# A ring of raw weight blocks in eight quarters instead of two whole blocks, in a one-core hybrid decoder layer

## The chip, the cores and the metric

The kernel runs on one core of one Trainium2 chip. The metric is the time of one execution on the device in microseconds, as a median of several runs; less is better. Beside the timed runs there is one profiled execution, whose trace is read here. The engines are named as in the profile: PE is TensorE, DVE is VectorE, ACT is ScalarE, POOL is GpSimd, SP is SyncE. SP issues most DMA transfers and computes nothing.

## What is computed

One layer of a decoder on 512 positions of width 1024, all in float32: an RMS norm, one wide input projection, two token mixers beside each other (a short gated convolution and a chunked gated delta rule with eight heads), a sigmoid-gated merge, an output projection, and a gated feed-forward part with a convolution over three positions.

```python
h = rmsnorm(x, norm_mix_g[l])
proj = h @ w_in[l]
bg, cg, xv, q, k, v, z, a, b, ga, gb = jnp.split(proj, pts, axis=-1)
y_a = short_conv_branch(bg, cg, xv, conv_a_w[l]) @ w_a_out[l]
y_b = gdn_branch(q, k, v, z, a, b, ...) @ w_b_out[l]
mix = jax.nn.sigmoid(ga) * y_a + jax.nn.sigmoid(gb) * y_b
x = x + mix @ w_o[l]
h = rmsnorm(x, norm_ffn_g[l])
x = x + conv_ffn(h, w_up[l], ffn_conv_w[l], w_down[l])
...
return rmsnorm(x, norm_final_g)
```

Nearly all of the arithmetic is in the products with `w_in`, `w_a_out`, `w_b_out`, `w_o`, `w_up` and `w_down`. Every weight is read from HBM once.

## The kernel before

**Products in three parts.** A float32 product is made of three matmuls in a rounded format (float32r): each operand is split into a rounded part and the rest (`wh` and `wl` for a weight, likewise for the activations), and `mm3` sums low x high, high x low and high x high (line 108 is the matmul in it).

**Blocks and jobs.** The weights are cut into blocks of 1 MB: 128 partitions by 16 tiles of 128 columns, or by four rows of 512. A list of jobs goes through them in order; `run_jobs` works one job at a time. A job has a block and a function `use` that issues its matmuls. There are three kinds of blocks:

- `Block`: four quarters, each split into `wh` (a cast on ACT, line 140) and `wl` (a subtraction on DVE, line 141).
- `SumBlock`: the block is used in a product scheme with seven instead of eight partial products. Its split has seven steps: quarters 0, 1 and 2 are split first ("11", "12", "22"), then DVE forms sums and differences in place in the same quarters (line 161, `to`), and four more parts are split from these: s3 from quarter 3, s2 from quarter 0, s4 from quarter 1 and s1 from quarter 2.
- `FormBlock`: rows for the products with `w_o` and `w_down`, loaded in one or two pieces (line 193). Those of `w_down` from the third on lie in buffers of their own (`raws`) and don't go through the ring.

**The ring.** The raw blocks lie in a ring with the tag `raw`: two slots of a whole block (16 KB a partition in all). A block is loaded by one DMA transfer of 1 MB on SP's queue (line 135). The tile framework lets a new tile into a slot when the last reader of the old tile is done, and places the waits itself. The first block (K of the first pair of heads) is already loaded in four pieces (line 419), into one tile. `wh` and `wl` have rings of `WQ` = 12 quarters each.

**The order.** In `run_jobs`, for job i: what is left of the split of block i is finished, the split of block i+1 is put into a queue that advances a step after every 2048 columns of matmuls, the load of block i+2 is issued, and then the matmuls of block i are issued. With these matmuls go the other queues' steps: PSUM results are taken out by ACT and DVE (in a `sum_job`, the copies `u` and `v` on lines 323 to 330 by ACT and the sums on lines 312 and 316 by DVE; the job's own later matmuls wait for the copies), and the delta rule's chains advance. The instructions of DVE, ACT, POOL and SP are put in order by a planner that simulates the engines and the transfers; in stretches under `manual_schedule` their order is the written one. Each engine, and SP's queue, works strictly in its order.

**The gate.** POOL issues a second kind of transfers, the sums of blocks of `w_o` and `w_down` that are formed in DRAM by accumulating transfers of 256 KB (line 1162). They are let in three at a time by `feed`, after each job from the middle of the kernel on: POOL copies one element of the raw block just being loaded (line 222), which makes it wait for the landing.

Of the kernel before, what the change touches and what calls it, by code (L numbers as in the profile page):

```python
# [9 lines left out]
F32 = mybir.dt.float32  # L10
F32R = mybir.dt.float32r
AF = mybir.ActivationFunctionType
ALU = mybir.AluOpType
# [3 lines left out]
P = 128  # L17
S = 512
# [8 lines left out]
C_BG, C_CG, C_XV, C_Q, C_K, C_V, C_Z, C_GA, C_GB = range(0, 36, 4)  # L27
# [33 lines left out]
def layer_kernel(ctx, tc, x, norm_mix_g, w_in, w_ab, conv_a_w, gdn_conv_w, gdn_A_log, gdn_dt_bias,  # L61
                 gdn_norm_g, w_a_out, w_b_out, w_o, norm_ffn_g, w_up, ffn_conv_w, w_down,
                 norm_final_g, out):
    nc = tc.nc
    pe, act, dve, pool = nc.tensor, nc.scalar, nc.vector, nc.gpsimd
# [6 lines left out]
    wp = ctx.enter_context(tc.tile_pool(name="wp", bufs=2))  # L72
# [3 lines left out]
    def nm(s):  # L76
        cnt[0] += 1
        return f"{s}{cnt[0]}"
# [8 lines left out]
    def advance(queue, n):  # L87
        while n and queue:
            queue[0].step()
            if queue[0].done:  # L90
                queue.popleft()
            else:
                n -= 1
# [28 lines left out]
            mm(o, ah, bh, False, i == n - 1, free)  # L122


    class Block:
        def __init__(self, src, quarter=(4, P)):
            self.src, self.quarter = src, quarter
            self.raw, self.ready, self.lead, self.fed = None, False, 2, True
            self.wh, self.wl = {}, {}

        def load(self):
            if self.raw is not None:
                return
            self.raw = wp.tile([P, 4, *self.quarter], F32, tag="raw", bufs=2, name=nm("raw"))
            nc.sync.dma_start(out=self.raw, in_=self.src())

        def part(self, name, src):
            wh = self.wh[name] = wp.tile([P, *self.quarter], F32R, tag="wh", bufs=WQ, name=nm("wh"))
# [4 lines left out]
        def split(self):  # L143
            if self.ready:
                return
            self.ready = True
            for q in range(4):
                self.part(q, self.raw[:, q])
                yield


# [1 line left out]
    class SumBlock(Block):  # L153
        def split(self):
            if self.ready:
                return
            self.ready = True
            r = [self.raw[:, q] for q in range(4)]

            def to(q, a, b, op):  # L160
                dve.tensor_tensor(out=r[q], in0=a, in1=b, op=op)  # L161

            self.part("11", r[0])
            yield
            self.part("12", r[1])
            yield
            self.part("22", r[2])
            yield
            to(2, r[3], r[2], ALU.add)
            to(3, r[0], r[3], ALU.subtract)  # L170
            self.part("s3", r[3])
            yield
            to(0, r[2], r[0], ALU.subtract)
            self.part("s2", r[0])
            yield
            to(1, r[1], r[0], ALU.subtract)
            self.part("s4", r[1])
            yield
            self.part("s1", r[2])
            yield  # L180


    class FormBlock(Block):
# [4 lines left out]
        def load(self):  # L188
            if self.raw is not None:
                return  # L190
            self.raw = self.place()
            for lo, hi, src in self.runs:
                nc.sync.dma_start(out=self.raw[:, lo:hi], in_=src)

        def split(self):
            if self.ready:
                return
            self.ready = True
            for q, name in enumerate(self.names):
                self.part(name, self.raw[:, q])  # L200
                yield

    def run_jobs(jobs):
        jobs[1][0].load()
        for i, (block, use) in enumerate(jobs):
            Task(block.split()).finish()
            drain(splits)
            if i + 1 < len(jobs):
                splits.append(Task(jobs[i + 1][0].split()))
            for j, (later, _) in enumerate(jobs[i + 2:i + 5]):  # L210
                if later.lead >= j + 2:
                    later.load()
            if adds and i + 2 < len(jobs) and jobs[i + 2][0].fed:
                feed(jobs[i + 2][0].raw)
            use(block.wh, block.wl)
# [2 lines left out]
    gate = const.tile([1, 64], F32, name="gate")  # L218

    def feed(raw):  # L220
        el = raw[0:1, 1].rearrange("p k n -> p (k n)") if len(raw.shape) == 4 else raw[0:1, 1]
        tc.keep_in_program_order(pool.tensor_copy(out=gate[:, 0:1], in_=el[:, 0:1]))  # L222
        advance(adds, FEED)

# [188 lines left out]
    tbd = [dram.tile([4, 8, 32, 32], F32, name=f"tbd{p}") for p in range(4)]  # L413

    k_block = Block(lambda: w_in[C_K])
    k_block.raw = wp.tile([P, 4, 4, P], F32, tag="raw", bufs=2, name=nm("raw"))

    def load_k(q):
        nc.sync.dma_start(out=k_block.raw[:, q], in_=w_in[C_K][:, 4 * q:4 * q + 4])

    HS = S // 2

# [6 lines left out]
    def ab_split():  # L429
        raw = ab_raw  # L430
        act.copy(out=ab2[:, :, 0:16], in_=raw)
        dve.tensor_tensor(out=ab2[:, :, 16:32], in0=raw, in1=ab2[:, :, 0:16].bitcast(F32), op=ALU.subtract)
# [44 lines left out]
    with tc.tile_pool(name="st1", bufs=1) as st1:  # L477
# [15 lines left out]
        load_x(0)  # L493
        load_x(1)
        load_k(0)
        wr = st1.tile([P, P], F32, name="wr")
        nc.sync.dma_start(out=wr[0:96], in_=gdn_conv_w.rearrange("o j (c p) -> (o j c) p", p=P))
        nc.sync.dma_start(out=wr[96:120], in_=conv_a_w.rearrange("o j (c p) -> (o j c) p", p=P))
        nc.sync.dma_start(out=wr[120:128], in_=norm_mix_g.rearrange("o (c p) -> (o c) p", p=P))
        ab_raw = st1.tile([P, ND, 16], F32, name="ab_raw")  # L500
        nc.sync.dma_start(out=ab_raw, in_=w_ab)
        load_k(1)
        load_x(2)
        load_x(3)
        load_k(3)
        load_k(2)
        dtb = gs.tile([P, H], F32, name="dtb")
# [54 lines left out]

        def round_k(q):
            wh = k_block.wh[q] = wp.tile([P, 4, P], F32R, tag="wh", bufs=WQ, name=nm("wh"))
            act.copy(out=wh, in_=k_block.raw[:, q])

        def rest_k(q):
            wl = k_block.wl[q] = wp.tile([P, 4, P], F32R, tag="wl", bufs=WQ, name=nm("wl"))
            dve.tensor_tensor(out=wl, in0=k_block.raw[:, q], in1=k_block.wh[q].bitcast(F32), op=ALU.subtract)


        def ab_tile(k):
# [11 lines left out]
        with tc.manual_schedule(engines={mybir.EngineType.DVE, mybir.EngineType.Activation, mybir.EngineType.Pool}):  # L584
# [4 lines left out]
            pe.transpose(out=po[:, 0:P], in_=wr, identity=ident)  # L589
            norm_x(1)  # L590
            round_k(0)
            dve.tensor_copy(out=wA, in_=po[:, 0:P])
            scale_x(1)
            turn_x(1, bs)
            busy(2, P)
            ab_split()
            round_k(1)
            rest_k(0)
            o_ab, o_k = bank(), [bank(), bank()]
            for ks in (lower, upper):  # L600
                for k in ks:
                    out_hi(0, bs, k)
                for k in ks:
                    out_lo(0, bs, k)
                    k_tile(0, k)
                    ab_tile(k)
                if ks is lower:
                    rest_k(1)
            norm_x(2)
            round_k(3)  # L610
            rest_k(3)
            scale_x(2)
            norm_x(3)
# [636 lines left out]
    def split_ya():  # L1250
        st["yas"] = [Rows([by_columns(page(n, "yas", F32R)) for n in names])
                     for names in (("kq0", "KU0"), ("AV0", "vT", "Dm"))]
        for k in range(ND):
            split(st["yas"], k, st["ya"][:, k, :])
            yield

    def split_yb():
        st["yb"] = [hp.tile([P, ND, S], F32R, tag=f"h{i}", name=f"yb{i}") for i in range(2)]
        for k in range(ND):
            split(st["yb"], k, yb[:, k, :])  # L1260
            yield
# [214 lines left out]
        return use  # L1476

    def raw():
        return wp.tile([P, 4, S], F32, tag="raw", bufs=2, name=nm("raw"))

    jobs += [(FormBlock(*o_w.first_pass(p), 2, raw), o_first(p)) for p in range(ND // 2)]
    jobs.append((FormBlock(*o_w.low(), 2, raw), o_low))
# [296 lines left out]
```

## Time and profile before

| what | value |
| --- | --- |
| median of 3 timed runs | 949.43 us (949.36 to 951.06) |
| profiled execution | 953.14 us, of which the span from first to last instruction is 951.3 us |
| granted TensorE clock, mean | 0.994 |
| PE, DVE, ACT, POOL busy | 98%, 82%, 57%, 18% of the span |
| ring loads on lines 135 and 193 | 65 of 1 MB in one transfer, and 9 more blocks in one or two transfers (rows of `w_o` and `w_down`) |
| DMA traffic | 138.17 MB, mean 145 GB/s |

A page of the profile gives busy time per engine, the span in slices, the chain of work that ended last, the costliest groups of instructions and the DMA issues. A row of the chain has a start, a duration and what ran. A row of a timeline has start and duration in us, engine, line, operation, output<-inputs, shapes and count; in square brackets stands how long the engine was idle before it and what it waited for. Rows of the timeline merge neighbours of one kind. A row of stretches has the stretch, its length, then for PE, weight loads, DVE, ACT and POOL the busy time with the count of instructions, then the granted TensorE clock, the busy share of the DMA engines and GB/s. A row of DMA issues has the queue, the count, the size and the median time from issue to landing. A row of one source line has durations (shortest, median, longest, in ns) and the first and last start. The end of a matmul is modelled, so the pace of the PE is read from starts.

### The profile page before, as it was taken

To read this page: it belongs to the slowest core of one execution; us is meant where nothing else is said; L and a number is where in the kernel's file an instruction comes from. 1 tells how busy PE (TensorE), PEld (TensorE's weight loads), DVE (VectorE), ACT (ScalarE), POOL (GpSimd) and SP (SyncE) were. 2 spreads that over 40 slices of the span, in tenths; PEclk is the share of its full clock that TensorE was granted. 3 is DMA by queue.
4 is the path that set the end of the run, shared out by engine and by line. 5 is a ranking of instruction groups with operands and counts; after the bars stand their busy time and mean duration, and the time that the engine had idled before them with its cause. 6 is when DMAs were issued, how large, how long until landed. Compare 5 with 4: busy or idle time off the path is not lost.

```text
span 951.3 us, 17103 instructions
## 1 busy us (share of the span) xinstructions
PE 936.8 (98%) x6512; PEld 828.4 (87%) x6512; DVE 779.3 (82%) x1448; ACT 545.7 (57%) x1202; POOL 171.4 (18%) x280
## 2 busy tenths in 40 slices
PE   8999999999999999999999999999999999999996
PEld 7888887987889999999888888998899998888885
DVE  5978686898978998999653479999899998969785
ACT  6896756666565645555642245556556556546463
POOL 3330401304110022222332000232222210000000
PEclk9999999999999999999999999999999999999999
DMA  6443412213021477666786545585755774177332
GB/s 230 156 141 98 121 54 90 76 54 98 9 91 46 120 200 160 174 203 165 237 232 151 126 143 191 176 206 189 198 123 206 172 175 136 45 264 234 101 133 89
DMA packets 51890, 138.17 MB, mean 145 GB/s; under 512 B 21691, under 2 KB 22624, under 8 KB 43104
## 3 DMA queue, kind: packets, MB, share of 16 engines
q1 hardware_dynamic: 39120, 107.45, 33.1%
q0 software_dynamic: 12544, 29.37, 16.6%
q8 instruction: 51, 0.84, 0.4%
q14 instruction: 31, 0.25, 0.1%
q10 hardware_dynamic: 144, 0.26, 0.1%
HBM read 133.64 MB, written 32.78 MB: 175 GB/s over the span
## 4 chain that ended last, share of the span: by engine, by line
PE 83%; DVE 7%; ACT 4%; DMA 3%; issue 2%; SPq 0%; POOL 0%; POOLq 0%; DVEq 0%; ACTq 0%
PE ps L108 75%; DVE wl L141 2%; DVE raw L161 2%; PE ps L739 1%; DMA raw<-in_w_in_dram 1%; ACT wh L140 1%; PE ps L774 1%; DMA raw<-in_w_a_out_dram 1%; DMA raw<-in_w_up_dram 1%; PE ps L977 1%; PE ps L997 1%; PE ps L986 1%; DVE c L352 1%; PE ps L965 0%; PE ps L964 0%
## 5 line engine op out<-in xcount | busy, mean ns | idle before, releaser
L140 ACT CAST wh<-raw 128x512 fp32r<-128x512 f32 x377 | 221.4, 620 | 182.8 <-PE ps L108 99.9
L141 DVE TENSOR_TENSOR wl<-raw,wh 128x512 fp32r<-128x512 f32 x377 | 251.1, 687 | 42.9 <-ACT wh L140 39.1
L108 PE MATMUL ps<-hT,wh 128*128 128x512 f32 (+1 forms) x1048 | 283.1, 350 | 0.8 <-ACT hT L555 0.5
L108 PEld LDWEIGHTS ps<-hT,wh 128*128 128x128 f32 x1048 | 183.4, 190 | 21.3 <-ACT hT L555 0.7
L108 PE MATMUL ps<-hT,wl 128*128 128x512 f32 (+1 forms) x524 | 172.6, 343 | 0.0
L108 PE MATMUL ps<-h,wh 128*128 128x256 f32 (+1 forms) x688 | 168.6, 333 | 0.0
L108 PEld LDWEIGHTS ps<-h,wh 128*128 128x128 f32 x688 | 118.5, 189 | 12.7 <-DVE h L1436 0.2
L108 PE MATMUL ps<-h,wl 128*128 128x256 f32 (+1 forms) x344 | 108.1, 332 | 0.0
L108 PEld LDWEIGHTS ps<-hT,wl 128*128 128x128 f32 x524 | 99.5, 190 | 9.7
L108 PE MATMUL ps<-ts,wh 128*128 128x256 f32 x544 | 102.5, 282 | 2.1 <-ACT v L326 1.9
L108 PE MATMUL ps<-wh,xs 128*128 128x512 f32 (+1 forms) x320 | 96.7, 384 | 0.0
L108 PEld LDWEIGHTS ps<-ts,wh 128*128 128x128 f32 x544 | 86.3, 191 | 2.7 <-ACT v L326 2.1
L161 DVE TENSOR_TENSOR raw<-raw 128x512 f32<-128x512 f32 x108 | 74.3, 688 | 1.8
L222 POOL COPY gate<-raw 1x1 f32<-1x1 f32 x38 | 21.4, 564 | 276.1 <-DMA raw<-in_w_up_dram 117.2
L108 PEld LDWEIGHTS ps<-h,wl 128*128 128x128 f32 x344 | 65.2, 189 | 6.3
L108 PEld LDWEIGHTS ps<-wh,xs 128*128 128x128 f32 x320 | 59.7, 188 | 11.9
L108 PE MATMUL ps<-ts,wl 128*128 128x256 f32 x272 | 66.7, 281 | 0.0
L108 PE MATMUL ps<-wl,xs 128*128 128x512 f32 (+1 forms) x160 | 61.5, 384 | 0.0
L108 PE MATMUL ps<-us,wh 128*128 128x256 f32 x320 | 58.1, 278 | 1.2 <-ACT v L326 1.2
L352 DVE SCALAR_TENSOR_TENSOR ct<-ps,wA,ct 128x511 f32<-128x511 f32 (+2 forms) x72 | 53.3, 742 | 4.0 <-ACT ct L349 3.9
L140 ACT CAST wh<-raws 128x512 fp32r<-128x512 f32 x66 | 38.9, 618 | 27.0 <-PE ps L108 9.4
L141 DVE TENSOR_TENSOR wl<-raws,wh 128x512 fp32r<-128x512 f32 x66 | 42.8, 687 | 13.4 <-ACT wh L140 13.4
(340 smaller groups left out, 1642.2 us busy)
## 6 DMA issues: line engine op xcount, KB each, us to landing
raw<-in_w_in_dram SPq DMA_DIRECT2D x35, 1024.0 KB, 5.3
raw<-in_w_up_dram SPq DMA_DIRECT2D x22, 1024.0 KB, 6.2
dv<-in_w_down_dram POOLq DMA_DIRECT2D x50, 256.0 KB, 6.0
raws<-dv SPq DMA_DIRECT2D x8, 768.0 KB, 6.0
ov<-in_w_o_dram POOLq DMA_DIRECT2D x20, 256.0 KB, 5.9
raws<-in_w_down_dram SPq DMA_DIRECT2D x10, 512.0 KB, 4.5
raw<-in_w_a_out_dram SPq DMA_DIRECT2D x4, 1024.0 KB
raw<-in_w_b_out_dram SPq DMA_DIRECT2D x4, 1024.0 KB, 5.8
```

The costliest lines, as they stand in the source:

```text
L108: pe.matmul(o, lhsT=a, rhs=b, start=start, stop=stop, skip_group_check=free)
L140: act.copy(out=wh, in_=src)
L141: dve.tensor_tensor(out=wl, in0=src, in1=wh.bitcast(F32), op=ALU.subtract)
L161: dve.tensor_tensor(out=r[q], in0=a, in1=b, op=op)
L222: tc.keep_in_program_order(pool.tensor_copy(out=gate[:, 0:1], in_=el[:, 0:1]))
L352: dve.scalar_tensor_tensor(out=dst[:, sh:], in0=src[:, :S - sh], scalar=wcol(j), in1=dst[:, sh:], op0=ALU.mult, op1=ALU.add)
L739: pe.transpose(out=o[:, n * P:(n + 1) * P], in_=src[:, n * P:(n + 1) * P], identity=ident)
L774: pe.matmul(o[:, i], lhsT=kqs[:, a, h, 0, sl], rhs=kqs[:, b, h, :, sl], start=a > 0, stop=a + b == 0)
L977: pe.matmul(o[:, 0:P], lhsT=TTf[:, f, :], rhs=rs[h], start=True, stop=True)
L986: pe.matmul(o2[:, 0:P], lhsT=kn[:, f, :], rhs=vns[h], start=True, stop=True)
L997: pe.matmul(o[:, 0:P], lhsT=A[:, f, :], rhs=vns[h], start=True, stop=True)
```

## The change

The ring `raw` gets eight slots of a quarter block (2 KB a partition each, 16 KB in all as before). `load` takes four tiles and issues four transfers of 256 KB, each into its own tile; a transfer waits for its own slot, and a cast or subtraction for its own quarter. `FormBlock` blocks that come through the ring are loaded quarter by quarter too. The first block's four transfers go into four tiles instead of parts of one. The gate on POOL copies an element of quarter 1's tile, where it copied one at the same place of the whole tile. All reads of `raw[:, q]` become reads of `raw[q]`.

```diff
+    def raw_tile(*quarter):
+        return wp.tile([P, *quarter], F32, tag="raw", bufs=8, name=nm("raw"))
+
...
-            self.raw = wp.tile([P, 4, *self.quarter], F32, tag="raw", bufs=2, name=nm("raw"))
-            nc.sync.dma_start(out=self.raw, in_=self.src())
+            self.raw = [raw_tile(*self.quarter) for _ in range(4)]
+            for q, t in enumerate(self.raw):
+                nc.sync.dma_start(out=t, in_=self.src()[:, 4 * q:4 * q + 4])
...
-                self.part(q, self.raw[:, q])
+                self.part(q, self.raw[q])
...
-            r = [self.raw[:, q] for q in range(4)]
+            r = self.raw
...
-                nc.sync.dma_start(out=self.raw[:, lo:hi], in_=src)
+                if isinstance(self.raw, list):
+                    for q in range(lo, hi):
+                        nc.sync.dma_start(out=self.raw[q], in_=src[:, q - lo])
+                else:
+                    nc.sync.dma_start(out=self.raw[:, lo:hi], in_=src)
...
-        el = raw[0:1, 1].rearrange("p k n -> p (k n)") if len(raw.shape) == 4 else raw[0:1, 1]
+        el = raw[1][0:1]
+        el = el.rearrange("p k n -> p (k n)") if len(el.shape) == 3 else el
...
-    k_block.raw = wp.tile([P, 4, 4, P], F32, tag="raw", bufs=2, name=nm("raw"))
+    k_block.raw = [raw_tile(4, P) for _ in range(4)]
...
-        return wp.tile([P, 4, S], F32, tag="raw", bufs=2, name=nm("raw"))
+        return [raw_tile(S) for _ in range(4)]
```

More of the change, by code (lines that the diff above doesn't have):

```diff
@@ L199, in split @@
             for q, name in enumerate(self.names):
-                self.part(name, self.raw[:, q])
+                self.part(name, self.raw[q] if isinstance(self.raw, list) else self.raw[:, q])
                 yield
@@ L415, in layer_kernel @@
     k_block = Block(lambda: w_in[C_K])
-    k_block.raw = wp.tile([P, 4, 4, P], F32, tag="raw", bufs=2, name=nm("raw"))
+    k_block.raw = [raw_tile(4, P) for _ in range(4)]
     def load_k(q):
-        nc.sync.dma_start(out=k_block.raw[:, q], in_=w_in[C_K][:, 4 * q:4 * q + 4])
+        nc.sync.dma_start(out=k_block.raw[q], in_=w_in[C_K][:, 4 * q:4 * q + 4])
     HS = S // 2
@@ L564, in round_k @@
             wh = k_block.wh[q] = wp.tile([P, 4, P], F32R, tag="wh", bufs=WQ, name=nm("wh"))
-            act.copy(out=wh, in_=k_block.raw[:, q])
+            act.copy(out=wh, in_=k_block.raw[q])
         def rest_k(q):
             wl = k_block.wl[q] = wp.tile([P, 4, P], F32R, tag="wl", bufs=WQ, name=nm("wl"))
-            dve.tensor_tensor(out=wl, in0=k_block.raw[:, q], in1=k_block.wh[q].bitcast(F32), op=ALU.subtract)
+            dve.tensor_tensor(out=wl, in0=k_block.raw[q], in1=k_block.wh[q].bitcast(F32), op=ALU.subtract)
         def ab_tile(k):
```

## The prediction

> **What bounds the kernel now.** I read the page first (busy times, chain that ended last), then the chain in order of time, and then each engine's timeline around the places where the chain leaves the PE.
>
> ```profile
> PE 936.8 (98%) x6512; PEld 828.4 (87%) x6512; DVE 779.3 (82%) x1448; ACT 545.7 (57%) x1202; POOL 171.4 (18%) x280
> PE 83%; DVE 7%; ACT 4%; DMA 3%; issue 2%; SPq 0%; POOL 0%; POOLq 0%; DVEq 0%; ACTq 0%
> ...
> 413.05 7.90 DMA raw<-in_w_in_dram
> 452.33 7.49 DMA raw<-in_w_a_out_dram
> 772.20 7.44 DMA raw<-in_w_up_dram
> ```
>
> TensorE is the bound: of the span of 951.3 us it is idle for 14.5. A faster loader can win back only idle time that a load causes, and time lost to a clock that such idle time lowers. The chain names three loads. The PE rows around them (two cut-outs of the timeline) show which of them cost anything:
>
> ```profile
> 455.65 0.28 PE L108 MATMUL ps<-ts,wl 128*128 128x256 f32 x1
> 455.77 0.28 PE L108 MATMUL ps<-ts,wh 128*128 128x256 f32 x1
> ...
> 459.31 0.64 PE L108 MATMUL ps<-hT,wh 128*128 128x256 f32 x4
> 461.88 0.55 PE L108 MATMUL ps<-ts,wh 128*128 128x256 f32 x1 [1.93 <-ACT v L326]
> 462.22 0.42 PE L108 MATMUL ps<-ts,wl 128*128 128x256 f32 x1
> 462.44 0.41 PE L108 MATMUL ps<-ts,wh 128*128 128x256 f32 x1
> ...
> 779.80 0.64 PE L108 MATMUL ps<-h,wh 128*128 128x256 f32 x4
> 781.65 0.39 PE L108 MATMUL ps<-us,wh 128*128 128x256 f32 x1 [1.20 <-ACT v L326]
> 781.87 0.28 PE L108 MATMUL ps<-us,wl 128*128 128x256 f32 x1
> ```
>
> Stall A: the PE stands for 1.93 us before 461.88, then starts a 256-column matmul every 0.22 us where it was 0.12 at 455. Stall B: 1.20 us before 781.65, and the pace afterwards is unchanged. The load at 413 costs the PE nothing. Both stalls name ACT's copy v, and ACT's own rows say why it is late:
>
> ```profile
> 459.90 1.66 ACT L140 CAST wh<-raw 128x512 fp32r<-128x512 f32 x3 [2.54 <-DMA raw<-in_w_a_out_dram]
> 461.46 0.36 ACT L326 COPY v<-ps 128x256 f32<-128x256 f32 x1
> 779.67 1.66 ACT L140 CAST wh<-raw 128x512 fp32r<-128x512 f32 x3 [3.38 <-DMA raw<-in_w_up_dram]
> 781.23 0.36 ACT L326 COPY v<-ps 128x256 f32<-128x256 f32 x1
> ```
>
> ACT works in order. Three casts of the next block stand ahead of the copy, and they wait 2.54 and 3.38 us for the whole block to land. The granted clock in stretches of 2 us gives the second half of A:
>
> ```profile
> 460.00:462.00 2.00, 0.12 (x1) 0.13 (x1) 1.45 (x3) 2.00 (x5) 1.60 (x4) 0.99 0.72 270
> 462.00:464.00 2.00, 2.00 (x10) 2.00 (x11) 1.07 (x2) 2.00 (x5) 1.65 (x4) 0.50 0.81 227
> 464.00:466.00 2.00, 2.00 (x13) 2.00 (x13) 0.49 (x1) 2.00 (x6) 0.61 (x2) 0.66 0.99 119
> ```
>
> At clocks of 0.50 and 0.66 (third number from the end) the PE loses 2 x 0.50 + 2 x 0.34 = 1.68 us. So A costs 1.93 + 1.68 = 3.61, B 1.20, together **4.81 us**. That is the whole prize.
>
> **The change part by part.** *Removed:* the wait of a block's load for the last reader of the block two before it. Now each quarter waits for one free slot. The two late loads follow blocks that are split in seven steps, whose DVE rows end as follows:
>
> ```profile
> 448.75 0.69 DVE L141 TENSOR_TENSOR wl<-raw,wh 128x512 fp32r<-128x512 f32 x1
> 449.36 0.69 DVE L161 TENSOR_TENSOR raw<-raw 128x512 f32<-128x512 f32 x1
> 449.96 4.14 DVE L141 TENSOR_TENSOR wl<-raw,wh 128x512 fp32r<-128x512 f32 x6
> ...
> 768.87 0.68 DVE L141 TENSOR_TENSOR wl<-raw,wh 128x512 fp32r<-128x512 f32 x1
> 769.48 0.68 DVE L161 TENSOR_TENSOR raw<-raw 128x512 f32<-128x512 f32 x1
> 770.85 2.00 DVE L141 TENSOR_TENSOR wl<-raw,wh 128x512 fp32r<-128x512 f32 x3 [0.69 <-ACT wh L140]
> ```
>
> By the order of that split, quarter 3 is last read for s3, quarter 0 by the last in-place subtraction and the cast pair of s2, quarter 1 for s4, quarter 2 for s1. At A the single load went out at 452.33. Quarters come free at about 449.4, 450.6, 451.3 and 452.3: head starts of about 2.9, 1.7, 1.0 and 0 us. At B the release of s3 is earlier still (before 768.87), then 770.2, 771.5, 772.2.
>
> *When the data are there.* The casts that hold up v need three quarters, and each now waits for its own landing only.
>
> ```profile
> raw<-in_w_in_dram SPq DMA_DIRECT2D x35, 1024.0 KB, 5.3
> raws<-df SPq DMA_DIRECT2D x6, 256.0 KB, 3.3
> raws<-in_w_down_dram SPq DMA_DIRECT2D x8, 256.0 KB, 8.2
> T<-tbd SPq DMA_DIRECT2D x16, 32.0 KB, 1.8
> ```
>
> A quarter of 256 KB lands 3.3 us after its issue in a quiet row and 8.2 in a crowded one; the whole block takes 5.3 at the median and 7.5 at A and B. I take 5, nearer to the quiet end, since three quarters together are less than the block that takes 7.5 there. Then A's third quarter (451.3) lands at 456.3, before the casts' turn (ACT idles from 457.36, 2.54 ahead of 459.90), and v ends at 457.36 + 1.66 + 0.36, about 459.3, ahead of the PE's need at 459.95. B: 771.5 + 5 = 776.5 against a turn at 776.29 and a need at 780.45. Both stalls go: **-4.81**.
>
> Bounds: if the slots are handed out in fixed turn, quarter 2 gets the slot of quarter 2, free only at 452.33, and lands no earlier than today. Then one cast instead of three follows the landing, and v comes 2 x 0.52 = 1.04 us earlier at each place (0.52 is the step from cast to cast, (1.66 - 0.62) / 2): gain **-2.1**. At best -4.81.
>
> *Added:* transfers. About 65 whole loads become four, and the few loads in two pieces become four as well: some 210 more issues on SP.
>
> ```profile
> L135 SPq DMA_DIRECT2D raw<-in_w_in_dram x35: 327/328/425, 13.3 to 443.7; - x35
> 92.24 1.79 SPq L835 DMA_DIRECT2D T<-tbd  x4
> L140 ACT CAST wh<-raw x377: 602/621/679, 22.9 to 827.8; 128x512 fp32r<-128x512 f32 x189
> L853 DVE STREAM_TRANSPOSE TT<-T x4: 436/438/441, 98.2 to 264.2; 128x256 f32<-128x256 f32 x4
> L141 DVEq EVENT_SEMAPHORE  x212: 21/21/809, 23.1 to 927.1; - x106
> 420.00:440.00 20.00, 20.00 (x174) 20.00 (x174) 19.36 (x32) 10.32 (x23) 6.09 (x10) 1.00 0.72 184
> ```
>
> An issue takes 328 ns (median), so the last quarter goes out about 1.0 us after the first when all four slots are free: early in the kernel, where the first load of whole blocks (13.3) is read by no cast before 22.9; hidden. What shares SP's queue can fall 1 us behind: T, issued at 92.24, is first transposed at 98.2, four us after its landing; hidden. If either cover went, it is 1 us once per place. Each cast and each subtraction gets its own wait, three more a block on ACT and on DVE, 0 to 21 ns each: at most 0.06 us a block where DVE (the 19.36 of 20 us in the stretch quoted) has 0.64 idle for two blocks. I charge **0**.
>
> The Trainium skill speaks against small transfers: "DMA: Bandwidth & Descriptors", section "Anatomy of one DMA", gives each a fixed cost near 2 us, and "Rules for kernel authors" asks for 1 MiB or more. By an estimate from that page, paid four times in a row this is 6 us more a block. The trace disagrees that it is paid in a row: four transfers of T go out within 1.79 us, and their landing time over all 16 is still 1.8 at the median.
>
> *Moved:* the gate. POOL's copy read an element after the whole block had landed; now it waits for quarter 1 only, so its three adds go out while quarters 2 and 3 may be under way. Today they meet the next load instead:
>
> ```profile
> 450.07 0.61 POOL L222 COPY gate<-raw 1x1 f32<-1x1 f32 x1 [8.59 <-DMA raw<-in_w_in_dram]
> 450.63 1.55 POOL L1162 DMA_DIRECT2D dv<-in_w_down_dram  x3
> ```
>
> The adds of 450.63 run into the load of 452.33 and are a reason for its 7.49. Two us earlier they would be mostly done by then; in exchange they may delay the previous block's second half, which is not read for several us. I take 0; the bounds are -1 (already inside A) and, as rival 2, a loss.
>
> **Sum and median.** The profiled execution took 953.14 (span 951.3 and 1.84 around it): 953.14 - 4.81 = 948.33. The median before, 949.43, is 3.71 below that execution, and 3.71 is close to all of A (3.61). So a timed run may have A without its clock loss, or not at all. With both stalls and half the clock loss in them the gain is 1.93 + 0.84 + 1.20 = 3.97: **945.5 us**. The clock loss full gives 944.6, none of it 946.3, the lower bound 947.3.
>
> The rule of "TensorE: Matmul & The Clock Gate" (the Trainium skill, Part 1, "What's actually happening") fits that doubt: activity is judged in free-running windows of about 3.4 us. By it the same 1.9 us of idling would lower the clock in one run and not in the next; this trace shows one case of each kind (A yes, B no, though B is shorter).
>
> **Rivals.**
> 1. *Another wait takes the place.* From 420 to 440 DVE is busy for 19.36 of 20 us, and steps of the split run on it between the PSUM work. With raw blocks there sooner, DVE is the next to be late and part of the idle time stays; or the timed runs never had A. Then only B goes: 949.43 - 1.20 = 948.2; with nothing gained 949.4. For it: the DVE row and the 3.71. Against: DVE itself idles behind the late load at A, since its rows wait for ACT's casts.
> 2. *Slower: the early gate.* POOL's adds join quarters 2 and 3 of every fed block. A crowded 256 KB takes 8.2 instead of 3.3, 4.9 more. From the point where this exceeds the head start (2.9 us at best) the casts, still ahead of v in ACT's order, wait longer than today: 2 us more at A and at B each, 949.43 + 4 = 953.4. For it: the collisions of today. Against: quarters 2 and 3 are in SP's queue before the gate can open.
> 3. *Transfers in a row* (the page's rule): four times 3.3 is 13.2 instead of 5.3, less 2.9: 5 us more at A and B, 959.4. Against: the T rows.
>
> **How the numbers follow.** Forecast (944.0 to 947.5): 0.52, and 0.03 for a larger gain. Rival 1 or nothing gained: 0.25. Rival 2: 0.18; rival 3: 0.02. A measurement of this kernel tells 0.2% (1.9 us) from no change, so below 947.5 is faster and above 951.3 slower: 0.55, 0.25, 0.20. The range takes in the larger gain, rival 1 and part of rival 2: 943.8 to 952.5; the likeliest case alone is 944.0 to 947.5.
>
> **What would show it.** Right: the PE rows have no idle time behind ACT v near 460 and 780, the slice 460 to 480 is back at clock 1.00, and the first casts of w_a_out's block wait for no DMA. Wrong: PE's idle total stays near 14.5, or new waits of ACT wh for raw stand ahead of a copy that the PE needs; or 256 KB loads of raw land later than 7.5 us after their issue behind POOL's adds.

## The result and the profile after

The changed kernel takes 955.04 us (median of 4 runs, 953.67 to 956.85), the kernel before 949.39 on the same chip (949.08 to 951.06): a ratio of 1.0057, 95% interval 1.0036 to 1.0078. It is slower by 5.6 us, against a forecast of 945.5 and outside the range of 943.8 to 952.5. Its profiled execution took 955.27, with a span of 953.6.

From the page of the changed kernel, the busy times and the loads of the ring on SP's queue:

```profile
PE 936.4 (98%) x6512; PEld 827.0 (87%) x6512; DVE 780.2 (82%) x1448; ACT 543.5 (57%) x1200; POOL 172.4 (18%) x280
...
raw<-in_w_in_dram SPq DMA_DIRECT2D x144, 256.0 KB, 3.5
raw<-in_w_up_dram SPq DMA_DIRECT2D x88, 256.0 KB, 3.4
raw<-in_w_a_out_dram SPq DMA_DIRECT2D x16, 256.0 KB, 6.8
```

These say little: the PE is busy as long as before, and most quarters land 3.4 to 3.5 us after their issue at the median, those of `w_a_out` after 6.8. Where the time went is read from landmarks, products that occur in both kernels. The rows below give them with the first and last start (line 748 after is line 739 before). First the kernel before:

```profile
L739 PE MATMUL ps<-ident,kq x64: 270/273/273, 45.6 to 224.9; 128*128 128x128 f32 x64
L739 PE MATMUL ps<-ident,vT x32: 270/273/327, 63.9 to 235.9; 128*128 128x128 f32 x32
L739 PE MATMUL ps<-ident,AV x32: 270/273/328, 138.4 to 309.9; 128*128 128x128 f32 x32
L108 PE MATMUL ps<-yas,wh x128: 388/389/390, 477.2 to 520.5; 128*128 128x512 f32 x128
L108 PE MATMUL ps<-wh,xs x320: 278/389/390, 837.8 to 943.9; 128*128 128x512 f32 x152, 128*128 128x256 f32 x8
```

The same landmarks in the changed kernel:

```profile
L748 PE MATMUL ps<-ident,kq x64: 270/273/280, 47.9 to 232.1; 128*128 128x128 f32 x64
L748 PE MATMUL ps<-ident,vT x32: 270/273/328, 72.3 to 242.9; 128*128 128x128 f32 x32
L748 PE MATMUL ps<-ident,AV x32: 270/272/332, 146.6 to 317.6; 128*128 128x128 f32 x32
L108 PE MATMUL ps<-yas,wh x128: 389/389/390, 480.9 to 524.2; 128*128 128x512 f32 x128
L108 PE MATMUL ps<-wh,xs x320: 277/389/390, 839.9 to 946.0; 128*128 128x512 f32 x152, 128*128 128x256 f32 x8
```

The lag of the changed kernel is 2.3 us at the first turn of kq (47.9 - 45.6), 8.4 at the first turn of vT (72.3 - 63.9), 7.7 at the last turn of AV, 3.7 at the first product with yas (stall A lies ahead of it: 4.0 won) and 2.1 at the products with xs (stall B and smaller ones: 1.6 won). So the gain of the prediction is there in this pair of traces, 5.6 us; and 8.4 us are lost ahead of it, all between 40 and 72 us. The two profiled executions differ by 2.1 us only (955.27 and 953.14) and the medians by 5.6, because the execution profiled before lies 3.7 us above its median; how much of the 5.6 us gain timed runs have is asked by experiments 9 to 12. Between 40 and 72 us the PE of the changed kernel waits twice, where the kernel before has no wait of the PE at all:

```profile
45.25 0.41 PE L711 MATMUL ps<-g,triu 128*128 128x32 f32 x2 [1.56 <-POOL g L707]
...
63.27 0.79 PE L108 MATMUL ps<-hT,wh 128*128 128x512 f32 x1 [3.96 <-DVE KU L769]
```

and the second wait lowers the granted clock (third number from the end, stretches of 2 us):

```profile
60.00:62.00 2.00, 0.00 (x0) 0.00 (x0) 1.49 (x3) 2.00 (x8) 0.00 (x0) 0.96 0.00 0
62.00:64.00 2.00, 0.73 (x2) 0.64 (x3) 2.00 (x6) 1.84 (x12) 0.00 (x0) 0.50 0.36 112
64.00:66.00 2.00, 2.00 (x7) 1.51 (x6) 1.90 (x8) 1.78 (x9) 1.86 (x1) 0.50 0.21 56
66.00:68.00 2.00, 2.00 (x6) 1.61 (x5) 2.00 (x8) 0.00 (x0) 0.15 (x1) 0.50 0.31 102
68.00:70.00 2.00, 2.00 (x9) 1.54 (x9) 0.77 (x2) 0.00 (x0) 1.82 (x3) 0.84 0.30 42
```

From 63.27 on the PE loses 0.73 x 0.50 + 2 x 0.50 + 2 x 0.50 + 2 x 0.16 = 2.7 us to the clock. 1.56 + 3.96 + 2.7 = 8.2 us. Without its wait the changed kernel would start the product with `g` at 43.69 (45.25 - 1.56), 0.4 us earlier than the kernel before (44.1), so the loss to explain is about 8.8 us, and 0.6 stays open.

**Where the first wait comes from.** ACT's timeline in the changed kernel, and below it the stores and loads on SP's queue ahead of it:

```profile
30.24 0.62 ACT L144 CAST wh<-raw 128x512 fp32r<-128x512 f32 x1 [4.62 <-DMA raw<-in_w_in_dram]
30.76 0.68 ACT L358 ACTIVATE ct<-ps,wA 128x512 f32<-128x512 f32 x1
31.34 0.22 ACT L684 ACTIVATE beta<-abv 128x32 f32<-128x32 f32 x1
...
24.21 1.80 SPq L483 DMA_DIRECT2D tbd<-T  x4
26.11 4.04 SPq L139 DMA_DIRECT2D raw<-in_w_in_dram  x8
```

In the kernel before, the convolution's and the gate chain's activations come first and the first cast of that block (the Z block of the first pair) stands behind them:

```profile
27.82 0.69 ACT L349 ACTIVATE ct<-ps,wA 128x512 f32<-128x512 f32 x1 [0.16 <-PE ps L108]
28.41 0.22 ACT L675 ACTIVATE beta<-abv 128x32 f32<-128x32 f32 x1
...
32.33 0.62 ACT L140 CAST wh<-raw 128x512 fp32r<-128x512 f32 x1 [0.88 <-DMA raw<-in_w_in_dram]
```

With quarters the planner put the cast of the first one ahead of this work. The quarter goes out at 26.11, behind four stores of T64; the cast waits 4.62 us for it, and `beta` starts 2.9 us later than before (31.34 against 28.41). The load itself is no later than before: there the whole Z block goes out at 27.53, but its cast stands behind. From `beta` a chain on POOL leads to `g`. Two of its rows in the changed kernel, and below them the last one in the kernel before:

```profile
37.41 2.03 POOL L702 TENSOR_SCALAR q<-q 128x32 f32<-128x32 f32 x1
44.39 0.81 POOL L707 TENSOR_SCALAR g<-g 128x32 f32<-128x32 f32 x1
...
40.13 0.29 POOL L698 TENSOR_SCALAR g<-g 128x32 f32<-128x32 f32 x1
```

`g` is there at 45.20 instead of 40.42, 4.8 us later. Of these, 2.9 come from the cast: the chain starts at 31.65 instead of 28.72. The other 1.9 come from the chain itself, which takes 13.6 us instead of 11.7, with single operations of up to 2.03 us. The PE used `g` only at 44.1 before, 3.7 us after it was there; the late cast alone would give `g` at about 43.35 (31.65 + 11.7), just in time for 43.69. So the wait of 1.56 us needs both. Why POOL's chain got longer, no run shows; in experiment 1, where it starts at 28.18, it takes 12.6 us.

**Where the second wait comes from.** In `front(0)`, the delta rule's first part for the first pair of heads, the planner put the eight exps of Dm (2.45 us) into the midst of ACT's squares. Rows of ACT and then of DVE, changed kernel:

```profile
54.99 2.45 ACT L665 ACTIVATE Dm<-Dm,negG 128x128 f32<-128x128 f32 x8
...
57.71 1.28 ACT L1061 ACT_TABLE_LOAD   x1
59.00 0.63 ACT L1061 ACTIVATE vT<-ct 128x512 f32<-128x512 f32 x1
...
59.79 0.68 ACT L358 ACTIVATE ct<-ps,wA 128x512 f32<-128x512 f32 x1
...
60.50 0.75 DVE L361 SCALAR_TENSOR_TENSOR ct<-ps,wA,ct 128x511 f32<-128x511 f32 x1 [2.08 <-ACT ct L358]
...
62.53 0.68 DVE L769 TENSOR_TENSOR KU<-ps,kdv 128x512 f32<-128x512 f32 x1
```

The convolution's activation `ct` (59.79) stands behind exps, table load and vT; DVE waits 2.08 us for it, and the second KU, which the PE's next product waits for, stands behind that on DVE. Before, DVE has the two KU at 52.93 and 54.31, and the exps come after them. That the quarters, ready earlier, are the planner's reason for either place is read from the two orders; no run looks into the planner.

**Stalls A and B.** The PE of the changed kernel has no wait at A's place, which lies at 464.5 to 467.3 here, and it keeps its clock (1.00 in every stretch from 456 to 468):

```profile
466.00:468.00 2.00, 2.00 (x20) 2.00 (x19) 1.40 (x3) 2.00 (x6) 0.66 (x2) 1.00 1.01 379
```

Near 780 the PE waits for 0.26 us. ACT still waits for a quarter there, and the copy v that the PE needs waits for DVE's aTb (ACT's rows, then the PE's):

```profile
778.36 0.62 ACT L144 CAST wh<-raw 128x512 fp32r<-128x512 f32 x1 [1.64 <-DMA raw<-in_w_up_dram]
...
783.31 0.37 ACT L335 COPY v<-ps 128x256 f32<-128x256 f32 x1 [1.79 <-DVE aTb L1532]
...
783.74 0.38 PE L108 MATMUL ps<-us,wh 128*128 128x256 f32 x1 [0.26 <-ACT v L335]
```

A load is at the head of this chain all the same. The first quarter of the block goes out at 769.37 and lands at 778.28, 8.9 us later; behind it come its cast, the convolution's activation on ACT and its sum on DVE, aTb and the copy v. So the late landing is still there, but it costs the PE 0.26 us where it was 1.20.

### The profile page after: what moved, and what is told of

Its sections match the earlier page's. It is cut to its first block, busy times and chain, and to the rows that moved or that the text cites. A ratio compares the mean times of both kernels' runs of the same rounds, so it can differ in the third digit from the quotient of the medians.

```text
span 953.6 us, 17708 instructions
## 1 busy us (share of the span) xinstructions
PE 936.4 (98%) x6512; PEld 827.0 (87%) x6512; DVE 780.2 (82%) x1448; ACT 543.5 (57%) x1200; POOL 172.4 (18%) x280
## 4 chain that ended last, share of the span: by engine, by line
PE 87%; DVE 5%; DMA 4%; ACT 2%; issue 1%; POOL 1%; SPq 0%; POOLq 0%; ACTq 0%; DVEq 0%
PE ps L108 81%; DMA raw<-in_w_in_dram 2%; PE ps L748 1%; DVE wl L145 1%; DVE ct L361 1%; PE ps L783 1%; DMA raw<-in_w_up_dram 1%; PE ps L986 1%; PE ps L1006 1%; ACT Dm L665 1%; PE ps L995 0%; PE ps L974 0%; PE ps L973 0%; PE ps L1440 0%; DMA Dm<-gtd 0%
## 5 line engine op out<-in xcount | busy, mean ns | idle before, releaser
L144 ACT CAST wh<-raw 128x512 fp32r<-128x512 f32 x377 | 223.7, 620 | 194.0 <-PE ps L108 93.8
L165 DVE TENSOR_TENSOR raw<-raw,raw 128x512 f32<-128x512 f32 x108 | 74.2, 688 | 2.0
L231 POOL COPY gate<-raw 1x1 f32<-1x1 f32 x38 | 15.2, 400 | 269.7 <-DMA raw<-in_w_up_dram 114.7
```

The costliest lines, as they stand in the source:

```text
L144: act.copy(out=wh, in_=src)
```

## The experiments

The theory after the comparison: the loss is the two new waits, and both come of ACT's new order, not of the transfers. The rivals: the small transfers themselves, and the early gate (rival 2 of the prediction).

**1. The four stores off SP's queue.** The changed kernel with

```diff
-            nc.sync.dma_start(out=tbd[p].rearrange(...
+            pool.dma_start(out=tbd[p].rearrange(...
```

> The changed kernel with one edit: the four stores of the zeroed T64 into tbd (line 483) go out on POOL's queue instead of SP's. In the changed kernel they stood ahead of the Z block's first quarter on SP's queue, until 25.56 us, and that quarter went out at 26.11. Theory 1 (the loss is one late quarter, behind those stores, whose cast ACT must do before the gate chain): the quarter goes out before 22, no ACT idle time of 4.62 us at 25 to 30, PE's stalls near 43 and 59 go, and with them the half clock after 59; by the two curves of PE progress 8 us are won back: 955.0 - 8 = about 947. Theory 2 (four transfers cost more than one, everywhere): within 2 us of the changed kernel, 953 to 957.

Measured: 951.79 us, ratio to the kernel before 1.0018 (1.0008 to 1.0028). The order of ACT, DVE and PE is that of the changed kernel. The wait for `g` and ACT's wait at 30 are gone; the PE's wait for KU is still there:

```profile
60.24 0.50 PE L108 MATMUL ps<-hT,wh 128*128 128x512 f32 x1 [3.35 <-DVE KU L769]
```

So the first wait needs the late quarter, and the second does not; the time lies between the two expectations. About two thirds of the loss (1.0057 to 1.0018) goes with it; the last section says why that is more than 1.56 us.

**2. The cast kept where it was written.** The changed kernel with the first cast of the Z block bound behind everything written ahead of it on ACT:

```diff
-            act.copy(out=wh, in_=src)
+            cast = act.copy(out=wh, in_=src)
+            if self.pinned and name == 0:
+                tc.keep_in_program_order(cast)
...
+    jobs[3][0].pinned = True
```

> The changed kernel with one edit: the cast of the Z block's first quarter (the one ACT waited 4.62 us for) is held behind everything written before it on ACT; the stores and the late load stay on SP's queue as in the changed kernel. Theory 1 says lateness hurts only because of the cast's place in ACT's order: the load is as late as before, but the copies and activations of the gate chain no longer wait, so about 947 to 949 as in the run with the stores moved. If the load's lateness alone is enough (the Z block itself is late for the PE), it stays at 953 to 957.

Measured: 949.24 us, ratio 0.9991 (0.9979 to 1.0002). The planner's order changes with it as a whole, and the squares stand in a row again: the waits at 45 and 63 are both gone. A new one has come, since the exps of Dm are ahead of vT on ACT and Dm lands late:

```profile
57.16 2.45 ACT L669 ACTIVATE Dm<-Dm,negG 128x128 f32<-128x128 f32 x8 [4.06 <-POOL Dm L661]
...
66.75 1.10 PE L752 MATMUL ps<-ident,vT 128*128 128x128 f32 x4 [2.44 <-ACT vT L1065]
```

One cast kept in its place, with the order that the planner makes from it, takes away the whole loss. The ring and the transfers are those of the changed kernel, so the loss is not their price. That the whole order changes with the edit leaves open which single move counts; experiments 1, 5 and 6 take the two waits apart.

**3. Four transfers into whole slots.** The kernel before with

```diff
-            nc.sync.dma_start(out=self.raw, in_=self.src())
+            for q in range(4):
+                nc.sync.dma_start(out=self.raw[:, q], in_=self.src()[:, 4 * q:4 * q + 4])
```

> The kernel before with one part of the change alone: a whole block has one slot of two as before, but is loaded by four transfers of 256 KB into it, so casts wait per quarter while slots come free as a whole. Theory 1: in ACT's order the Z block's first cast stands behind the first convolution again, but two casts stand ahead of the gate chain's third activation, so a small part of the early loss, 0 to 3 us; stalls A and B (near 460 and 780) shrink by the earlier landing of the first quarters at most by half, since the slot comes free as late as before: 947 to 952. Theory 2 (transfers cost): 953 to 957 like the changed kernel.

Measured: 952.51 us, ratio 1.0025 (1.0011 to 1.0038). The split of the transfers alone is 0.25% slower, and wins nothing: with whole slots the late quarters go out when the block did (452.88 to 454.20 at A, 771.13 to 772.45 at B, against 452.33 and 772.20), and at B the PE now waits twice, 1.34 us at 777.93 and 0.68 at 781.72, against 1.20 before. Its trace has two more waits of the PE that the first trace of before does not have, 0.82 us at 47.20 for G from DVE and 0.81 at 718.25 for v from ACT. So four transfers without the finer slots are not free; how much of it is the transfers and how much the planner's order is not separated.

**4. The kernel before, again.**

> The kernel before, unchanged, for a second profile and the scatter of its time. If stall A with its half clock (3.6 us) is in every execution, this profile has it too and its profiled time is near 953. If it comes and goes, the profile shows a span nearer to 948 with PE's idle time smaller near 460. Ratio 1.000 within 0.002.

Measured: 949.61 us, ratio 0.9998 (0.9986 to 1.0011). Its profiled execution took 953.46, again some 4 us over the median. The order of ACT, DVE and PE is that of the first trace, and the clock at A is 1.00 (stretch from 462 to 464). The nearest wait of the PE is another one than A, 24 products ahead of it and for the copy u (the PE's row, then ACT's):

```profile
460.93 0.39 PE L108 MATMUL ps<-ts,wh 128*128 128x256 f32 x1 [1.32 <-ACT u L323]
...
455.50 1.14 ACT L140 CAST wh<-raw 128x512 fp32r<-128x512 f32 x2 [1.51 <-DMA raw<-in_w_in_dram]
459.99 0.63 ACT L1236 ACTIVATE mixa<-mixa 128x512 f32<-128x512 f32 x1 [2.04 <-DVE mixa L316]
461.31 1.13 ACT L140 CAST wh<-raw 128x512 fp32r<-128x512 f32 x2
```

The copy u stands behind mixa, which waits for DVE, and DVE is late behind the casts of the `w_in` block ahead (issued at 446.11, landed 9.3 us later). The casts of the block of `w_a_out` (461.31) wait for no transfer: stall A is not in this trace. So the 3.85 us by which this execution lies over its median are not A.

**5. The exps behind the squares.** The changed kernel with

```diff
-        if pr == 0:
-            exps(0)
-        Dm = Dms.pop(pr)
+        Dm = Dms.pop(pr) if pr else Dms[0]
...
+        if pr == 0:
+            exps(0)
+            Dms.pop(0)
         dve.tensor_scalar(sk, ssk, EPS, None, op0=ALU.add)
```

> The changed kernel with one edit: in front(0) the eight exps of Dm are written behind the eight squares of the first turn, not ahead of them. The order of ACT then has all squares in a row ahead of the exps, as in the kernel before; the early cast of the Z block's first quarter stays ahead of the gate chain. Theory (two new waits of the PE in the first 60 us, made by ACT's order): the PE's 4.0 us wait at 59 for the second KU and the half clock behind it (some 3.3 us) go, the 1.6 us wait at 43 stays: 955.0 - 5 to 7, so 948 to 950. Rival (the small transfers or the early gate slow the whole kernel): 954 to 956.

Measured: 948.64 us, ratio 0.9996 (0.9982 to 1.0010). The wait for KU is gone, the wait for `g` is still there (0.99 us), and the first turn of vT is at 65.5 instead of 72.3. The second wait with its clock was the larger part, some 6 us.

**6. Both edits.** The changed kernel with the edits of 1 and 5.

> The changed kernel with both edits: the four stores of T64 go out on POOL's queue, and the exps of Dm are written behind the squares. Theory of the two waits: neither the wait at 43 nor that at 59 is left, stalls A and B stay gone; against the 951.8 of the first edit alone the 3.4 us wait and its clock loss go: 946 to 949. Rival (what is left beyond the first edit comes from the transfers): no change against the first edit, 951 to 953.

Measured: 945.94 us, ratio 0.9967 (0.9955 to 0.9979): faster than either kernel. From 42 to 74 the PE has no gap and full clock; one of the four stretches of 8 us:

```profile
58.00:66.00 8.00, 8.00 (x41) 6.64 (x40) 6.73 (x12) 6.85 (x22) 5.18 (x8) 1.00 0.54 132
```

The last row of products with xs runs to 936.3, where the kernel before has 943.9 in its first trace, which lies 3.7 us over the median.

**7. The gate on the last quarter.** The changed kernel with

```diff
-        el = raw[1][0:1]
+        el = raw[3][0:1]
```

> The changed kernel with the gate of POOL's fed transfers reading an element of the block's last quarter instead of its second, so that nothing of POOL's goes out before the whole block has landed, as in the kernel before. Theory of the two waits: the gate has no part in it, 954 to 956, with the lag of some 8 us already there at 60 us. The rival of the prediction (early gate, POOL's transfers ahead of the block's own last quarters): some 4 us faster, 950 to 952.

Measured: 955.08 us, ratio 1.0067 (1.0052 to 1.0082). No change from the changed kernel, both waits are there (1.54 and 4.14 us). The early gate has no part in the loss.

**8. Dm on another queue.** The kernel of 2 with G's store and the first load of Dm on POOL's queue:

```diff
-        nc.sync.dma_start(out=Dm, in_=gtd[8 * pr:8 * pr + 8, :].partition_broadcast(P))
+        (nc.sync if pr else pool).dma_start(out=Dm, in_=gtd[8 * pr:8 * pr + 8, :].partition_broadcast(P))
...
-        nc.sync.dma_start(out=gtd, in_=GT)
+        pool.dma_start(out=gtd, in_=GT)
```

> The changed kernel with the Z block's first cast kept behind all that is written ahead of it on ACT, and with G's store and the first load of Dm on POOL's queue instead of behind the quarters on SP's. With the first edit alone (949.2) the PE still waited 2.4 us at 64 for vT, which stood on ACT behind exps that waited 4.1 us for Dm. Theory: Dm lands some 3 us earlier, that wait goes with its clock loss: 945.5 to 947.5. Rival (vT is late for another reason): 949 to 950.

Measured: 952.21 us, ratio 1.0034 (1.0022 to 1.0046), slower than the kernel of 2. The expectation does not hold: Dm is past SP's queue and is still as late. POOL's rows, the issue and then the operation that reads Dm:

```profile
49.81 0.60 POOL L660 DMA_DIRECT2D Dm<-gtd  x1 [3.13 <-DMA gtd<-GT]
...
56.15 1.10 POOL L661 TENSOR_SCALAR_AFFINE_SELECT Dm<-Dm 128x1024 f32<-128x1024 f32 x1 [5.73 <-DMA Dm<-gtd]
```

It is read 6.3 us after its issue, with nine quarters issued on SP between 43.75 and 54.7. On SP's queue in the kernel of 2, with quarters around it too, it was the same 6.3 us (49.76 to 56.03). In the kernel of 6, where the quarters around it go out before 43.8 and after 51.4, it is issued at 47.15 and read at 50.99, 3.8 us later; in the changed kernel, with no quarter issued from 46.95 to 55.5, 3.6 us later (50.22 to 53.85). The queue was not the cause; that the quarters under way slow Dm down is the reading that is left. It fits these four traces, and no run changes that alone.

**9 and 10. The prize alone.** In the kernel before, the block whose late landing makes stall A takes its data from the slot of the block ahead of it, and its load is left out; in the second kernel the same is done at B too. All other orders stay the same, but for one cast each.

```diff
+            if self.same is not None:
+                self.raw = self.same.raw
+                return
             self.raw = wp.tile([P, 4, *self.quarter], F32, tag="raw", bufs=2, name=nm("raw"))
...
+        if g == 0:
+            jobs[-1][0].same = jobs[-2][0]
```

> The kernel before with one load left out: the first block of w_a_out, whose late landing makes stall A, takes its raw weights from the slot of the block ahead of it, which has long landed (so this block's product is not the reference's). All other orders stay the same but for one cast and one load. In the profile stall A (2 to 4 us in two executions of the kernel before) must go under every theory. If timed executions have A as the profiled one has it: 3 to 4 us faster, 945.5 to 946.5. If A is mostly missing from them, as the 3.7 us between the profiled execution and the median suggest: 948.5 to 949.5, no change that can be told.

> As the run before it, and the w_up block whose late landing makes stall B takes its raw weights from the slot ahead of it too (two products are not the reference's). This is the whole prize of the predicted change without anything of its cost. With A and B in timed executions: 944 to 945.5. With B alone: some 1.2 us below the median before, 947.5 to 948.5. With neither: no change.

Measured: without A's load 950.00 us, ratio 1.0005 (0.9997 to 1.0014); without both 947.06, ratio 0.9982 (0.9970 to 0.9994). The first is no gain. Its profile has no wait at A; the wait for the copy u at 448, 0.18 us in the first trace of before (at 446.91), is 0.72 here, and B is longer than its 1.20:

```profile
448.39 0.38 PE L108 MATMUL ps<-ts,wh 128*128 128x256 f32 x1 [0.72 <-ACT u L327]
...
779.68 0.38 PE L108 MATMUL ps<-us,wh 128*128 128x256 f32 x1 [1.53 <-ACT v L330]
```

ACT's casts ahead of that u wait 0.70 us for the `w_in` block. So what A's load costs in timed runs is either not there or given back at such places: at most 0.3 us is won (the lower end, 0.9997). Without both loads the trace has no wait of the PE above 0.20 us from 440 to 786. The whole prize is 1.7 us (0.6 to 2.8), against the 3.97 that the prediction took.

**11. The two edits without the ring.** The kernel before with the edits of 1 and 5; the order of ACT, DVE and PE is that of the kernel before.

> The kernel before with the two edits that took the new waits out of the changed kernel (stores of T64 on POOL's queue, exps of Dm written behind the squares); ring and transfers as before. If the 945.9 of the changed kernel with both edits owes its gain to the ring of quarters: 948.5 to 950. If the edits themselves are worth it: 946 to 947.

Measured: 949.47 us, ratio 1.0000 (0.9988 to 1.0012). The edits are worth nothing without the ring of quarters. Its profiled execution took 948.88, near the median, and has nothing of A: the casts of that block wait for no transfer, and the clock is 1.00. The PE waits 0.53 us for the copy u, at the product of experiment 4's wait (456.53).

So of three traces of this order (the first of before, 4 and 11) only the first has stall A.

**12. Both edits once more**, beside 9 to 11.

> The changed kernel with both edits once more, beside the three runs above on the same chip: 0.25 to 0.45% below the kernel before.

Measured: 945.79 us, ratio 0.9967 (0.9955 to 0.9979), as in 6. In its profiled execution (948.56, the longest of its six) B is there with waits of 0.99 and 0.75 us; in that of 6 it isn't. The block's first quarter lands 10.7 us after its issue here (761.15 to 771.85) and 5.7 us after it in 6 (760.13 to 765.82). So the ring of quarters does not take B away in every execution.

## Why the prediction was wrong

**The step that failed** is "Added", with its charge of 0 and the cover it names: early in the kernel "the first load of whole blocks (13.3) is read by no cast before 22.9; hidden". That holds for this load. The Z block's, which stands behind four stores on the same queue, was not looked at. And the cost was not an issue or a landing but an order. With quarters the planner gave the cast of the Z block's first quarter an earlier place on ACT and put the exps of Dm amid the squares, and work that the PE needs stands behind both. The prediction let only the gate move and took ACT's old order for granted, at A and B too, though a planner makes it. Shown in its place: two waits of the PE, 1.56 and 3.96 us, and 2.7 us of clock. Cost: 8.2 us in the profile; in timed runs the two edits take the ratio from 1.0057 to 0.9967, 8.5 us.

**The removed wait** was right in kind. The quarters of w_a_out's block go out at 456.98, 458.18, 459.05 and 459.80, steps of 1.2, 0.9 and 0.75 where the prediction had 1.2, 0.7 and 1.0; no cast of theirs waits for a transfer, and v is in time. At B the quarters go out at 769.37, 773.26, 774.64 and 775.20; with the lag of 3 us there the prediction's times are before 771.9, then 773.2, 774.5 and 775.2. From issue to landing the four took 8.9, 6.5, 5.8 and 5.9 us at B and 3.7 to 5.4 at A, where 5 was assumed: at B the loads are slower than the prediction had them, and the first one is the late one. The cover for DVE's and ACT's extra waits held: no new wait of the PE at the split of a block is to be seen in this trace. B itself did not go in every execution (experiment 12).

**The size of the prize** was too large. The prediction took 3.97 from one trace, noted that the median lay 3.71 below it, and read the difference as A or its clock. Part of it is something else. That trace loses clock at the kernel's start too, 2 x 0.15 + 4 x 0.35 = 1.70 us:

```profile
10.00:12.00 2.00, 1.29 (x6) 1.04 (x7) 1.21 (x4) 2.00 (x7) 0.00 (x0) 0.85 0.97 379
12.00:16.00 4.00, 4.00 (x25) 3.74 (x25) 3.56 (x10) 4.00 (x9) 0.95 (x1) 0.65 0.74 222
```

Of the fourteen traces only three have this loss: before, 4 and 12, and these three executions lie 3.7, 3.9 and 2.8 us over the medians of their kernels. The first turn of kq stands at 45.6 and 46.2 in before and 4, at 44.7 in 11; at 46.2 in 12, at 45.2 in 6: 0.9 to 1.5 us. So the excess is neither A alone nor A's clock alone, and the whole of it is not explained. Of the 77 later timed executions of the kernel before, 73 show a mean granted clock of 0.997 to 0.999 and none the 0.994 of the first trace. The reading "not at all", which the prediction gave to rival 1, is the nearest for A: experiment 9 finds nothing to win there, and the traces of 4 and 11 do not have it. What stays is near the 948.2 of rival 1: 947.06 for both loads removed, 947.7 by its ratio (949.4 x 0.9982). The ring with both edits gains 3.1 us (2.0 to 4.3), more than this prize by its median; the intervals overlap, so a gain beyond A and B isn't shown. That 945.9 is near the 945.5 forecast is no support for its sum.

**The rivals.** Rival 2 gave the right side for a wrong reason: experiment 7 takes the early gate away and nothing changes. Rival 3 (transfers in a row) is refuted for its size: a quarter takes 3.4 to 3.5 us (6.8 for `w_a_out`), a block took 5.3, and with quarters and a good order on ACT the kernel is faster than with blocks. The page behind it, the Trainium skill's "DMA: Bandwidth & Descriptors" ("Anatomy of one DMA" and "Rules for kernel authors"), has a fixed cost near 2 us for each transfer and asks for 1 MiB or more. It does not say that this cost is paid in a row, and its section measured transfers that GpSimd issues, while the ring's loads go out on SP. The fourth way, that the planner's order elsewhere changes, was not among them.

## What to carry to other kernels

Where a planner orders engines that work strictly in their order, a change of what becomes ready when is a change of every engine's order, far from the place it is meant for; before a forecast, ask for each early piece what it can now overtake, and whether its data come in time there. A stall in one profiled execution is a prize only if other executions have it. A second profile of the unchanged kernel can tell: here it lacked the stall and lay as far over the median as the first, so the distance from the median alone says nothing of one stall; look for other losses in it, such as the one at the start. A loss by the order, as here in the changed kernel, can be repaired in the order, by a position for one or two operations, without giving up the change.

## What the runs showed of the hardware

**The loss of clock comes in steps.** In these traces, outside the last microseconds of the span, the clock falls to a half for a stretch of 3.41 us or twice that, and so costs 1.70 or 3.40 us. Between two changes of the clock lie whole multiples of 3.41 us: 447.15 us in the first trace of before (131 times 3.41), 54.61 in the changed kernel (16 times). After the 3.35 us wait of experiment 1 it is once, by these three stretches:

```profile
60.00:62.00 2.00, 1.76 (x6) 1.49 (x7) 1.90 (x7) 1.87 (x10) 0.90 (x1) 0.82 0.43 135
62.00:64.00 2.00, 2.00 (x6) 1.51 (x6) 2.00 (x9) 0.80 (x5) 1.13 (x1) 0.50 0.41 126
64.00:66.00 2.00, 2.00 (x9) 1.59 (x8) 1.76 (x6) 0.00 (x0) 0.93 (x2) 0.83 0.09 15
```

0.36 + 1.00 + 0.34 = 1.70. At stall A of the first trace it is 0.02 + 1.00 + 0.68 = 1.70, and after the 3.96 us of the changed kernel 0.08 + 3 x 1.00 + 0.32 = 3.40.

**The length of one wait does not decide it.** 1.93 us (before, stall A) and 2.44 us (experiment 2) brought one stretch, as 3.35 us did; 1.32 (experiment 4), 1.53 (9) and 1.56 us (the changed kernel at 45) brought none. What fits all fourteen traces is a grid of 3.41 us, lying differently in each execution, and the PE's busy time in the last part of the grid ahead of a change. Half clock followed where the PE was busy for 0.81 us (experiment 8), 0.90 (changed kernel), 0.97 (2), 1.04 (1), 1.18 (7), 1.48 (before, A) and, at the kernel's start, 1.82 (12), 1.86 (before) and 1.99 us (4). It did not follow at 1.99 us (8, at the start), 2.06 (3, at B), 2.09 and 2.13 (4) or 2.21 us (before, B). So in these traces the line lies near 2.0 of 3.41 us; the ends of matmuls are modelled, so it is not sharper. In the changed kernel the next part of the grid (61.82 to 65.24) again had 1.97 us, and a second half-clock stretch followed: that is why its 3.96 us cost twice what the 3.35 us cost.

This is also why experiment 1 wins more than 1.56 us. It takes that wait away, shortens the other by 0.6, and has one stretch of half clock instead of two. Of the changed kernel's 3.40 us, 0.7 falls into the wait itself, so the clock costs its PE 2.7 us, against 1.7 in experiment 1: 1.56 + 0.6 + 1.0 = 3.2 of the 3.7 us between the ratios.

"TensorE: Matmul & The Clock Gate" of the Trainium skill (Part 1, "What's actually happening") has free-running windows of about 3.4 us, which fits this grid. That a drop takes a whole idle window does not fit it, since the PE was busy for up to 1.99 us of the part ahead of a drop. The prediction's reading by this page, that the same idling lowers the clock in one run and not in the next, is borne out at the kernel's start by experiments 6 and 12: one kernel, and only 12 has the drop.
